# Fourteen modulation loads with buffers from the start, and the relative-bias staging moved to the fourth block of stage 1

## The chip, the cores and the metric

The kernel runs on one core of one Trainium2 chip. The metric is the time of one execution on the device in microseconds (us); the kernel before was run three times.

## What is computed

One layer of a streaming trunk, in float32, for a prompt of 2048 tokens and eight sample streams of 16 tokens. Cut to what matters here:

```
m = silu(c) @ w_mod + b_mod                  # six sections of 1024 columns; sections 0 and 1 are needed first
h = rmsnorm(x) * (1 + scale1) + shift1
proj = h @ w_in                              # columns shared out between two groups
group A: causal conv of width 4 + silu on q, k, v; gated delta rule; gated norm
group B: banded attention, scores + rel_bias[:, clip(qpos - kpos)]
x = x + gate1 * (concat(o_A, o_B) @ w_out)
x = x + gate2 * relu(norm(x) * (1 + scale2) + shift2) ** 2 @ w_down     # through w_up
```

## The kernel before

The program has two stages. Stage 1 goes over six blocks of two or three tiles of 128 tokens (`BLOCKS1`; the third tile of the first block holds the samples). Stage 2 does the attention, the output projection and the FFN. A scheduler in the framework orders the instructions of each engine from the code's order and its own model of times; the order is fixed when the program is built. Large matrices are multiplied in three matmuls of split halves (lines 162 to 164, or three lines of their own in a group's loop), so each weight tile is loaded (`raw`, L174), cast by ScalarE (`w`, L175), and its low half is made by GpSimd (`w`, L82 on POOL). In the first block the cast weights are also stored (`s_w_in`, L183), and later blocks load them back (L178) beside fresh `raw` loads.

All loads and stores of this case are issued by SyncE (SP), in one queue in program order. An issue waits for what its buffer needs and, through one of eight semaphores used in turn, for the DMA issued eight before it.

**The start.** `modulation_start` loads sixteen pieces of `w_mod` of 512 KB (`raw` on L281). Each pair of pieces feeds eight matmuls into `mps` (L287), an add into `rows` (L82), and small transposes `ptm` (L316). Nine buffers (`NPRE`) hold the pieces, so the tenth load waits until the first piece has been multiplied. The three `x` tiles of the first block are loaded on L260, after every fourth piece. `conv_consts` then loads three groups of conv weights and histories (`cwt`, two small DMAs each, L450 and L451), transposes each in eight small matmuls (`psc`, L454 and L455), and copies them out on VectorE (`cw`, `hists`). When the modulation and these are done, `htmp`/`hT` are made, and TensorE starts with `psg` (264 columns, the gates) and `psq` (384 columns, q/k/v for the conv).

**Each block.** The conv of group A is VectorE and ScalarE work per column group (`pre`, `hist`, `y`); the delta rule of each block runs in generators that the scheduler mixes with the next projections. The `x` tiles of the next block are loaded (L372) and normed (`bst` is the statistics of a tile on VectorE, L377) ahead of time.

**The relative biases.** `rel_bias` runs once, when block index 1 begins. It loads 8 rows (`ext`, L1095), reverses and extends them by two copies on VectorE (L1097, L1098), stores them (`s_ext`, L1099), and spreads them by two DMAs from DRAM to DRAM: `s_bias`, 2560 KB (L1100), and `s_bs`, 264 KB (L1101). Stage 2 reads these.

Of the kernel before, what the change touches and what calls it, by code (L numbers as in the profile page):

```python
# [8 lines left out]
F32 = mybir.dt.float32  # L9
# [5 lines left out]
P = 128  # L15
D = 1024
# [19 lines left out]
NT2 = max(len(b) for b in BLOCKS2)  # L36
LATE = (4, 2)
GP = 3
NPRE = 9


def bcast(ap, axis, n):
# [9 lines left out]
class Trunk:  # L52
# [167 lines left out]
    def modulation_start(self, first, tiles, p0):  # L220

        nc, i = self.nc, self.i
        R = 1 + NB
        self.modT = self.const.tile([P, 4, KT, R], F32, name="modT")
        self.cT = self.p1.tile([P, KT, 32], F32, name="cT")
        crow = p0.tile([P, D], F32, name="crow")[0:R]
        nc.sync.dma_start(crow[0:1], i["c_prompt"])
        nc.sync.dma_start(crow[1:R], i["c_sample"])
        load = lambda n: self.mod_load(*first[n], p0.tile([P, D], F32, tag="raw0", name="raw0", bufs=NPRE))
        rvs, xs = [], []  # L230
        for n in range(min(NPRE, len(first))):
            rvs.append(load(n))
            if n == 1:
                gains = p0.tile([16, P], F32, name="gains")
                nc.sync.dma_start(gains[0:8], i["norm1_g"][0].rearrange("(a b) -> a b", b=P))
                nc.sync.dma_start(gains[8:16], i["norm2_g"][0].rearrange("(a b) -> a b", b=P))
                rows = p0.tile([P, 2, D], F32, name="rows")
                nc.gpsimd.memset(rows, 0.0)
                for k, sec in enumerate(dict.fromkeys(c[0] for c in first)):
                    nc.sync.dma_start(rows[0:R, k], dram_ap(i["b_mod"], sec * D, [[0, R], [1, D]]))  # L240
        th = p0.tile([P, D], F32, name="cth")[0:R]
        self.act(th, crow, AF.Tanh, scale=0.5)
        self.ts(crow, crow, 0.5, ALU.mult)
        self.stt(crow, th, 1.0, crow, ALU.add, ALU.mult)
        pt = self.pa.tile([P, 512], F32, tag="pa", name="pt")
        for k in range(KT):
            nc.tensor.transpose(pt[:, k * R:(k + 1) * R], crow[:, k * P:(k + 1) * P], self.ident[0:R, 0:R])
        nc.vector.memset(self.cT, 0.0)
        nc.vector.tensor_copy(self.cT[:, :, 0:R], pt[:, 0:KT * R].rearrange("p (k r) -> p k r", r=R))
        self.rowT = self.const.tile([P, 16], F32, name="rowT")  # L250
        pr = self.pa.tile([P, 512], F32, tag="pa", name="ptr")
        nc.tensor.transpose(pr[:, 0:16], gains, self.ident[0:16, 0:16])
        nc.vector.tensor_copy(self.rowT, pr[:, 0:16])
        order = list(dict.fromkeys(c[0] for c in first))
        for n, (sec, q, u) in enumerate(first):
            if n + NPRE < len(first):
                rvs.append(load(n + NPRE))
            if n % 4 == 3 and len(xs) < len(tiles):
                x = self.hp.tile([P, D], F32, tag="x", name="x", bufs=self.nx)
                nc.sync.dma_start(x, self.x_src(tiles[len(xs)]))  # L260
                xs.append(x)
            if u == 0:
                ps = self.gp.tile([P, 512], F32, tag="g", name="mps")[:, 0:256]
            self.mod_mm(ps, rvs[n], u, u == 0, u == 1)
            if u:
                row = rows[:, order.index(sec), q * 256:(q + 1) * 256]
                self.tt(row, row, ps, ALU.add)
                self.mod_finish(sec, q, row, self.gp, "g")
        self.conv_consts(p0)
        return xs  # L270
# [168 lines left out]
    def conv_consts(self, p0):  # L439
        nc, c, i = self.nc, self.p1, self.i  # L440

        self.cw = c.tile([P, 12, 4], F32, name="cw")
        self.hist = c.tile([P, 12, 3], F32, name="hist")
        nc.vector.memset(self.hist, 0.0)
        self.hists = c.tile([P, 12, NB * 3], F32, name="hists")
        for g in range(3):
            gs = slice(g * 512, (g + 1) * 512)
            t = p0.tile([24, D], F32, tag="cwt", name="cwt", bufs=3)
            w4, h24 = t[0:4, 0:512], t[0:24, 512:1024]
            nc.sync.dma_start(w4, i["conv_w"][0][:, gs])  # L450
            nc.sync.dma_start(h24, i["state_conv"][0].rearrange("b w c -> (b w) c")[:, gs])  # L451
            ps = self.pa.tile([P, 512], F32, tag="pa", name="psc")
            for k in range(4):
                nc.tensor.transpose(ps[:, k * 4:(k + 1) * 4], w4[:, k * P:(k + 1) * P], self.ident[0:4, 0:4])  # L454
                nc.tensor.transpose(ps[:, 64 + k * 24:64 + (k + 1) * 24], h24[:, k * P:(k + 1) * P], self.ident[0:24, 0:24])  # L455
            self.ts(self.cw[:, 4 * g:4 * g + 4], ps[:, 0:16].rearrange("p (k r) -> p k r", r=4), 0.5, ALU.mult)
            nc.vector.tensor_copy(self.hists[:, 4 * g:4 * g + 4], ps[:, 64:160].rearrange("p (k r) -> p k r", r=24))
# [570 lines left out]
    def phase1(self):  # L1028
        nc, tc = self.nc, self.tc
        with ExitStack() as st:  # L1030
            P_ = lambda name, **kw: st.enter_context(tc.tile_pool(name=name, bufs=1, **kw))
            right = ExitStack()
            R_ = lambda name, bufs=1, **kw: right.enter_context(tc.tile_pool(name=name, bufs=bufs, side="right", **kw))
            self.p1, self.hp, self.qp = (P_(x) for x in ("p1c", "p1h", "p1q"))
            self.bp = R_("p1b")
            self.ps = R_("p1ps", 3, space=bass.MemoryType.PSUM)
            pst = ExitStack()
            self.pa = pst.enter_context(tc.tile_pool(name="p1pa", bufs=5 - GP, side="right", space=bass.MemoryType.PSUM))
            self.patag = "pa"
            self.nt = max(len(b) for b in BLOCKS1)  # L1040
            self.nx, self.nA, self.inplace = 3, 4, True
            self.hT = self.p1.tile([P, KT, 2, self.nt * P], F32R, name="hT1")
            with tc.tile_pool(name="p0", bufs=1, side="right") as p0:
                xs = self.modulation_start([(sec, q, u) for q in range(4) for sec in (1, 0) for u in range(2)],
                                           BLOCKS1[0], p0)
            self.mod_todo = [(sec, q, u) for sec in (2, 3, 4, 5) for q in range(4) for u in range(2)]
            self.tp = R_("p1t")
            self.cp = pst.enter_context(tc.tile_pool(name="p1a", bufs=1, side="right"))
            self.phase1_consts()
            S0 = self.tp.tile([P, AH, P], F32, tag="S", name="S", bufs=1)  # L1050
            nc.vector.memset(S0, 0.0)
            self.S = S0
            B = BLOCKS1
            ca = lambda b: 24 * (512 + 1536) * len(B[b])
            cb = lambda b: 24 * 1536 * len(B[b])
            last = len(B) - 1
            self.load_hT(B[0], xs, 0, 1)
            for bi, tiles in enumerate(B):
                self.bi = bi
                self.keep["w_in"] = bi == 0  # L1060
                if bi == 1:
                    self.rel_bias()
                self.drain_to(bi - 2)
                blk = self.proj_a(tiles, self.hT, B[bi + 1] if bi in LATE else ())
                if bi == last:
                    break
                self.gdn(blk, tiles, bi)
                self.pace(0.95 * (cb(bi) * (bi not in LATE) + ca(bi + 1)), 6000)
                if bi not in LATE:
                    self.proj_b(tiles, self.hT, B[bi + 1])  # L1070
            pst.close()
            self.pa = R_("p1pa2", 1, space=bass.MemoryType.PSUM)
            self.ap2 = R_("p1att", 1, space=bass.MemoryType.PSUM)
            self.ap = R_("p1at")
            self.queue(self.attention_first(BLOCKS2[0]), 1 + BH + BH // 2 * len(BLOCKS2[0]) + BH + 2, lane=2)
            self.queue(self.conv_gen(), 6, lane=1)
            self.gdn(blk, tiles, last)
            rest = [last] + list(LATE)
            self.pace(0.85 * sum(cb(b) for b in rest))
            for b, nb in zip(rest, rest[1:] + [None]):  # L1080
                self.proj_b(B[b], self.hT, B[nb] if nb is not None else ())
            self.drain()
            nc.sync.dma_start(self.o["gdn_prompt"][0, 0].rearrange("h k v -> k h v"), self.S)
            right.close()
# [506 lines left out]
```

## Time and profile before

| | |
|---|---|
| median of 3 runs | 3227.69 us (3222.45 to 3229.71) |
| the profiled execution | 3216.33 us, span 3214.6 us |
| TensorE busy, share of the span | 95% |
| VectorE, ScalarE, GpSimd | 56%, 46%, 19% |
| mean granted TensorE clock | 0.979 of full speed |
| DMA | 751.69 MB, mean 234 GB/s |

The profile is one execution. It was 11.4 us faster than the median of the three timed runs, so a sum of changes is made against 3216.33 us and then carried to the median. PE is TensorE's matmul part, DVE VectorE, ACT ScalarE, POOL GpSimd, SPq the queue of SyncE. The granted clock is given as a share of full speed: 1.00 is 2.4 GHz and 0.50 is 1.2 GHz.

### The profile page before, as it was taken

The page shows a single profiled execution, that of the slowest core. Times are in us where ns is not written, and L with a number is a line of the kernel's source. Part 1 is how long each engine was busy: PE and PEld are TensorE (multiplying, and loading weights), DVE is VectorE, ACT ScalarE, POOL GpSimd, SP SyncE. Part 2 cuts the span into 40 slices and gives each one's busy share as a digit, 9 for nine tenths or more (in the row PEclk, how much of TensorE's full clock was granted, in tenths as well). Part 3 has the DMA queues.
Part 4 walks back from the last instruction along what each step waited for, and adds up shares of the span by engine and source line. Part 5 has one row for each costly group of instructions (what it writes and reads, how often), then busy time and mean ns, then how long its engine had stood idle before and what let it go on. Part 6 is the DMA issues. An engine that isn't in the chain of part 4 may idle for free.

```text
span 3214.6 us, 53090 instructions
## 1 busy us (share of the span) xinstructions
PE 3059.3 (95%) x19577; PEld 2704.5 (84%) x19577; DVE 1805.8 (56%) x4526; ACT 1479.9 (46%) x2707; POOL 599.3 (19%) x521
## 2 busy tenths in 40 slices
PE   7899999999999979989999999999999999998998
PEld 5798988898989968878888888888888887787997
DVE  5975777767868654778225556244556433243223
ACT  3554544556655645655434435344434433333332
POOL 4641312121222247631122210000000000000000
PEclk9999999999989989989999999999999999999999
DMA  9789897878897778884655666566675676677876
GB/s 292 221 269 280 265 291 220 269 234 254 270 305 248 233 239 264 258 293 157 193 191 190 208 227 216 178 198 194 197 254 186 214 228 222 224 245 227 254 245 197
DMA packets 630268, 751.69 MB, mean 234 GB/s; under 512 B 59680, under 2 KB 483728, under 8 KB 627960
## 3 DMA queue, kind: packets, MB, share of 16 engines
q1 hardware_dynamic: 624248, 716.84, 70.4%
q0 software_dynamic: 5760, 31.46, 2.9%
q8 instruction: 154, 2.52, 0.3%
q14 instruction: 106, 0.87, 0.1%
HBM read 635.55 MB, written 115.52 MB: 234 GB/s over the span
## 4 chain that ended last, share of the span: by engine, by line
PE 70%; DMA 13%; DVE 11%; issue 2%; ACT 2%; POOL 2%; SPq 1%; ACTq 0%; POOLq 0%; DVEq 0%
PE psu L1479 7%; PE psd L164 7%; PE psd L162 7%; PE psu L1480 7%; PE psu L1481 7%; PE psd L163 7%; DMA x<-in_x_prompt_dram 2%; PE psb L163 2%; PE psb L162 2%; PE psb L164 2%; PE psq L520 1%; PE psq L521 1%; PE psq L519 1%; PE psS L1267 1%; PE pv L1285 1%
## 5 line engine op out<-in xcount | busy, mean ns | idle before, releaser
L175 ACT CAST w<-raw 128x1024 fp32r<-128x1024 f32 (+1 forms) x528 | 552.5, 1048 | 356.4 <-PE psd L164 178.1
L1479 PE MATMUL psu<-hT,w 128*128 128x512 f32 (+2 forms) x1304 | 467.9, 360 | 5.6 <-ACT hT L104 5.6
L1480 PE MATMUL psu<-hT,w 128*128 128x512 f32 (+2 forms) x1304 | 466.6, 358 | 1.9 <-DVE r L89 1.4
L1481 PE MATMUL psu<-hT,w 128*128 128x512 f32 (+2 forms) x1304 | 465.4, 357 | 0.6 <-POOL w L82 0.6
L162 PE MATMUL psd<-w,u 128*128 128x512 f32 x1088 | 431.2, 396 | 0.7 <-DVE u L82 0.7
L164 PE MATMUL psd<-w,u 128*128 128x512 f32 x1088 | 429.8, 396 | 0.0
L163 PE MATMUL psd<-w,u 128*128 128x512 f32 x1088 | 426.6, 392 | 0.0
L82 POOL TENSOR_TENSOR w<-raw,w 128x1024 fp32r<-128x1024 f32 (+1 forms) x132 | 317.6, 2415 | 301.5 <-ACT w L175 232.4
L79 DVE SCALAR_TENSOR_TENSOR psu<-psu,r 128x512 f32<-128x512 f32 (+2 forms) x160 | 98.8, 617 | 417.0 <-ACT r L92 417.0
L82 DVE TENSOR_TENSOR y<-y,psd 128x512 f32<-128x512 f32 x238 | 162.5, 685 | 251.2 <-PE psd L164 250.5
L1479 PEld LDWEIGHTS psu<-hT,w 128*128 128x128 f32 x1304 | 245.4, 189 | 39.2 <-ACT hT L104 6.5
L1481 PEld LDWEIGHTS psu<-hT,w 128*128 128x128 f32 x1304 | 245.8, 189 | 33.7 <-POOL w L82 0.8
L1480 PEld LDWEIGHTS psu<-hT,w 128*128 128x128 f32 x1304 | 246.0, 189 | 33.3 <-DVE hT L82 2.5
L92 ACT ACTIVATE r<-psu 128x512 f32<-128x512 f32 (+2 forms) x160 | 85.5, 534 | 375.6 <-issue 209.8
L164 PEld LDWEIGHTS psd<-w,u 128*128 128x128 f32 x1088 | 204.2, 188 | 46.6 <-DVE u L82 0.3
L163 PEld LDWEIGHTS psd<-w,u 128*128 128x128 f32 x1088 | 204.6, 188 | 45.7 <-issue 1.9
L162 PEld LDWEIGHTS psd<-w,u 128*128 128x128 f32 x1088 | 204.4, 188 | 44.1 <-DVE u L82 1.5
L162 PE MATMUL psb<-w,hT 128*128 128x256 f32 x816 | 236.1, 290 | 0.4 <-ACT qraw L976 0.4
L164 PE MATMUL psb<-w,hT 128*128 128x256 f32 x816 | 234.1, 288 | 0.5 <-DVE hT L82 0.5
L163 PE MATMUL psb<-w,hT 128*128 128x256 f32 x816 | 233.3, 287 | 0.0
L519 PE MATMUL psq<-hT,w 128*128 128x384 f32 (+1 forms) x576 | 193.2, 336 | 0.9 <-ACT pres L534 0.9
L520 PE MATMUL psq<-hT,w 128*128 128x384 f32 (+1 forms) x576 | 193.3, 336 | 0.0
(318 smaller groups left out, 6566.7 us busy)
## 6 DMA issues: line engine op xcount, KB each, us to landing
raw<-in_w_up_dram SPq DMA_DIRECT2D x160, 512.0 KB
raw<-in_w_down_dram SPq DMA_DIRECT2D x160, 512.0 KB
raw<-in_w_in_dram SPq DMA_DIRECT2D x156, 512.0 KB
w<-s_w_in SPq DMA_DIRECT2D x130, 512.0 KB
w<-s_w_down SPq DMA_DIRECT2D x128, 512.0 KB
w<-s_w_up SPq DMA_DIRECT2D x96, 512.0 KB
raw<-in_w_out_dram SPq DMA_DIRECT2D x40, 512.0 KB
x<-in_x_prompt_dram SPq DMA_DIRECT2D x38, 512.0 KB
```

Of the source, the lines that this page charges most:

```text
L79: (eng or self.nc.vector).scalar_tensor_tensor(out, in0, scalar, in1, op0, op1)
L82: (eng or self.nc.vector).tensor_tensor(out, in0, in1, op)
L92: self.nc.scalar.activation(out, in_, func, **kw)
L162: mm(out, lh, rh, start=first, stop=False)
L163: mm(out, lh, rl, start=False, stop=False)
L164: mm(out, ll, rh, start=False, stop=last)
L175: nc.scalar.copy(w[:, 0, 0:n], r)
L519: mm(ps[:, 0:T], wh, hT[:, k, 0, 0:T], start=(k == 0), stop=False)
L520: mm(ps[:, 0:T], wh, hT[:, k, 1, 0:T], start=False, stop=False)
L1479: mm(ps[:, c0:c1], wh, h2[:, k, 0, c0:c1], start=(k == 0), stop=False)
L1480: mm(ps[:, c0:c1], wh, h2[:, k, 1, c0:c1], start=False, stop=False)
L1481: mm(ps[:, c0:c1], wl, h2[:, k, 0, c0:c1], start=False, stop=(k == KT - 1))
```

## The change

Three things change in the code of the start, and one in the loop over blocks. `NPRE` goes from 9 to 12, and two more pieces of `w_mod` go into the two buffers of another pool (tag `big`), so fourteen loads are issued without a wait for a buffer, and the last two after the first and the second multiplication. The three `x` loads are issued between them. The conv constants have one buffer in place of three (`cwt`), and the scratch `cth` of the silu shares it. And `rel_bias`, whose `ext` uses a buffer of the tag `big` too, is called at block index 3 instead of 1.

```
-NPRE = 9
+NPRE = 12
...
-        load = lambda n: self.mod_load(*first[n], p0.tile([P, D], F32, tag="raw0", name="raw0", bufs=NPRE))
         rvs, xs = [], []
-        for n in range(min(NPRE, len(first))):
-            rvs.append(load(n))
+
+        def load(n):
+            pool, tag, bufs = (self.hp, "big", 2) if n in (NPRE, NPRE + 1) else (p0, "raw0", NPRE)
+            rvs.append(self.mod_load(*first[n], pool.tile([P, D], F32, tag=tag, name="raw0", bufs=bufs)))
+
+        for n in range(min(NPRE + 2, len(first))):
+            load(n)
+            if n % 4 == 3 and len(xs) < len(tiles):
+                x = self.hp.tile([P, D], F32, tag="x", name="x", bufs=self.nx)
+                nc.sync.dma_start(x, self.x_src(tiles[len(xs)]))
+                xs.append(x)
...
-        th = p0.tile([P, D], F32, name="cth")[0:R]
+        th = p0.tile([24, D], F32, tag="cwt", name="cth", bufs=1)[0:R]
...
-            if n + NPRE < len(first):
-                rvs.append(load(n + NPRE))
-            if n % 4 == 3 and len(xs) < len(tiles):
-                x = self.hp.tile([P, D], F32, tag="x", name="x", bufs=self.nx)
-                nc.sync.dma_start(x, self.x_src(tiles[len(xs)]))
-                xs.append(x)
             if u == 0:
                 ps = self.gp.tile([P, 512], F32, tag="g", name="mps")[:, 0:256]
             self.mod_mm(ps, rvs[n], u, u == 0, u == 1)
+            if n + NPRE + 2 < len(first):
+                load(n + NPRE + 2)
...
-            t = p0.tile([24, D], F32, tag="cwt", name="cwt", bufs=3)
+            t = p0.tile([24, D], F32, tag="cwt", name="cwt", bufs=1)
...
-                if bi == 1:
+                if bi == 3:
                     self.rel_bias()
```

The change adds four lines ahead of most of the code, so a line of the kernel before stands four higher afterwards (L450 becomes L454).

SyncE's queue at the start. Before, the conv constants (`cwt`) are issued among the `w_mod` pieces, soon after the `x` tiles:

```order
L260 DMA x<-in_x_sample_dram 128x1024
L450 DMA cwt<-in_conv_w_dram 4x512
L451 DMA cwt<-in_state_conv_dram 24x512
L450 DMA cwt<-in_conv_w_dram 4x512
L451 DMA cwt<-in_state_conv_dram 24x512
L281 DMA raw_169<-in_w_mod_dram 128x4x256
L450 DMA cwt<-in_conv_w_dram 4x512
L281 DMA raw_176<-in_w_mod_dram 128x4x256
L451 DMA cwt<-in_state_conv_dram 24x512
```

The same queue of the changed kernel, from the last piece of `w_mod` on; five small constants (gdng, qkg twice, alog, dtb) stand between the first pair of `cwt` loads and the first rows of `w_in`, and are not shown:

```order
L174 DMA raw<-in_w_in_dram 128x4x264 x2
L174 DMA raw<-in_w_in_dram 128x8x128
L454 DMA cwt<-in_conv_w_dram 4x512
L455 DMA cwt<-in_state_conv_dram 24x512
L183 DMA s_w_in<-w 128x1056
L454 DMA cwt<-in_conv_w_dram 4x512
L455 DMA cwt<-in_state_conv_dram 24x512
L174 DMA raw<-in_w_in_dram 128x8x128
```

All sixteen pieces and the three `x` tiles now stand ahead of any `cwt` load; the second `cwt` group stands behind three `w_in` loads, and the third behind a store that waits for GpSimd.

VectorE, around the statistics (`bst`) of the third `x` tile of the second block. Before, they stand after the first group of the conv (`hist`, `y`):

```order
L529 COPY hist<-pre 128x3
L535 COPY hists<-pres 128x24
L79 SCALAR_TENSOR_TENSOR y<-pre,cw,y 128x256
L79 SCALAR_TENSOR_TENSOR y<-pres,cw,y 128x128
L79 SCALAR_TENSOR_TENSOR y<-pre,cw,y 128x256
L79 SCALAR_TENSOR_TENSOR y<-pres,cw,y 128x128
L79 SCALAR_TENSOR_TENSOR y<-pre,cw,y 128x256
L79 SCALAR_TENSOR_TENSOR y<-pres,cw,y 128x128
L527 COPY pre<-hist 128x3
L533 COPY pres<-hists 128x8x3
L377 BN_STATS bst<-x 128x6 x2
L79 SCALAR_TENSOR_TENSOR sgw<-th,psg 128x256
```

In the changed kernel:

```order
L79 SCALAR_TENSOR_TENSOR sgw<-th,psg 128x256
L381 BN_STATS bst<-x 128x6 x2
L382 BN_AGGR bmv<-bst 128x2
L82 TENSOR_TENSOR hT_98<-htmp,hT_98 128x4x128
L382 BN_AGGR bmv<-bst 128x2
L79 SCALAR_TENSOR_TENSOR ss<-bmv 128x1 x2
L89 TENSOR_SCALAR r<-ss 128x1 x2
L79 SCALAR_TENSOR_TENSOR sgw<-th,psg 128x256
L533 COPY hist<-pre 128x3
L539 COPY hists<-pres 128x24
```

The third statistics now stand ahead of the first conv group, and ahead of one `hT` of the first block.

SyncE's queue where the third block ends and the fourth begins. Before:

```order
L281 DMA rawx<-in_w_mod_dram 128x4x256 x2
L501 DMA s_sg<-sgw 128x256
L296 DMA mrow<-in_b_mod_dram 9x256
L560 DMA s_vt<-kvw 128x128 x3
L178 DMA w<-s_w_in 128x1024
L501 DMA s_sg<-sgw 128x256
L281 DMA rawx<-in_w_mod_dram 128x4x256
L174 DMA raw<-in_w_in_dram 128x8x128
L560 DMA s_kt<-kvw 128x128 x3
L372 DMA x<-in_x_prompt_dram 128x1024
```

In the changed kernel:

```order
L285 DMA rawx<-in_w_mod_dram 128x4x256
L1103 DMA s_ext<-ext 8x768
L285 DMA rawx<-in_w_mod_dram 128x4x256
L505 DMA s_sg<-sgw 128x256
L1104 DMA s_bias<-s_ext 1024x1x640
L1105 DMA s_bs<-s_ext 128x1x528
L300 DMA mrow<-in_b_mod_dram 9x256
L564 DMA s_vt<-kvw 128x128 x3
L285 DMA rawx<-in_w_mod_dram 128x4x256
L505 DMA s_sg<-sgw 128x256
L564 DMA s_kt<-kvw 128x128 x3
L376 DMA x<-in_x_prompt_dram 128x1024
```

The two DRAM to DRAM transfers now stand ahead of `mrow` and of the first `x` load of the fourth block (`rawx` are later pieces of `w_mod`; `mrow` is their bias row).

## Rows read from the trace of the kernel before

**Rows 1.** The page: the span, and busy time with shares and instructions of each engine.

```profile
span 3214.6 us, 53090 instructions
...
PE 3059.3 (95%) x19577; PEld 2704.5 (84%) x19577; DVE 1805.8 (56%) x4526; ACT 1479.9 (46%) x2707; POOL 599.3 (19%) x521
```

**Rows 2.** Windows: length; busy PE, PEld, DVE, ACT, POOL (instructions); granted clock; DMA share; GB/s.

```profile
20.00:40.00 20.00, 15.07 (x124) 8.90 (x115) 10.26 (x37) 7.69 (x10) 3.71 (x4) 0.97 0.96 296
40.00:60.00 20.00, 12.74 (x76) 11.18 (x77) 17.12 (x33) 8.94 (x16) 9.47 (x7) 0.69 0.84 274
...
80.00:100.00 20.00, 13.81 (x71) 13.18 (x70) 19.85 (x53) 9.64 (x22) 12.38 (x7) 0.91 0.71 216
...
220.00:320.00 100.00, 100.00 (x765) 88.37 (x764) 60.92 (x178) 51.05 (x101) 10.90 (x14) 1.00 0.96 294
```

**Rows 3.** The chain that ended last, first 140 us: start, length, what.

```profile
14.35 9.48 DMA raw<-in_w_mod_dram
...
61.76 13.64 DMA x<-in_x_prompt_dram
```

**Rows 4.** SyncE's timeline at the start: start, length, queue, line, operation.

```profile
16.25 0.34 SPq L450 DMA_DIRECT2D cwt<-in_conv_w_dram  x1
...
29.99 3.15 SPq L174 DMA_DIRECT2D raw<-in_w_in_dram  x3
...
35.45 0.37 SPq L281 DMA_DIRECT2D raw<-in_w_mod_dram  x1
...
49.06 1.90 SPq L1100 DMA_DIRECT2D s_bias<-s_ext  x1
51.01 8.12 SPq L1101 DMA_DIRECT2D s_bs<-s_ext  x1
...
61.76 5.70 SPq L372 DMA_DIRECT2D x<-in_x_prompt_dram  x1
```

**Rows 5.** TensorE's timeline at the start; in brackets idle before and what ended it.

```profile
25.68 0.26 PE L454 MATMUL psc<-ident,cwt 4*128 4x4 f32 x1 [0.85 <-DMA cwt<-in_conv_w_dram]
...
41.65 1.08 PE L287 MATMUL mps<-raw,cT 128*32 128x256 f32 x8 [2.88 <-DMA raw<-in_w_mod_dram]
...
48.03 0.57 PE L162 MATMUL psg<-w,hT 128*128 128x264 f32 x1
```

**Rows 6.** ScalarE's timeline, its first instruction.

```profile
3.16 1.28 ACT L92 ACT_TABLE_LOAD   x1 [3.16 <-DMA crow<-in_c_sample_dram]
```

**Rows 7.** VectorE's timeline, 40 to 76 us.

```profile
40.33 2.60 DVE L1097 COPY ext<-ext 8x320 f32<-8x320 f32 x1 [2.16 <-DMA ext<-in_rel_bias_dram]
42.85 2.48 DVE L1098 COPY ext<-ext 8x384 f32<-8x384 f32 x1
...
67.79 1.60 DVE L529 COPY hist<-pre 128x3 f32<-128x3 f32 x1 [6.87 <-ACT pre L528]
...
75.42 1.28 DVE L377 BATCH_NORM_STATS2 bst<-x 128x6 f32<-128x512 f32 x2 [3.77 <-DMA x<-in_x_prompt_dram]
```

**Rows 8.** SyncE's timeline where the third block ends.

```profile
495.42 0.46 SPq L501 DMA_DIRECT2D s_sg<-sgw  x1
500.12 0.31 SPq L296 DMA_DIRECT2D mrow<-in_b_mod_dram  x1
...
504.48 0.38 SPq L281 DMA_DIRECT2D rawx<-in_w_mod_dram  x1
...
507.43 0.41 SPq L372 DMA_DIRECT2D x<-in_x_prompt_dram  x1
```

**Rows 9.** Windows while `s_bias` moves, and at the end of the third block.

```profile
48.00:60.00 12.00, 10.07 (x61) 9.39 (x62) 9.50 (x25) 5.51 (x11) 4.34 (x4) 0.82 0.82 260
496.00:516.00 20.00, 19.11 (x223) 15.81 (x222) 13.73 (x42) 8.65 (x20) 6.52 (x6) 1.00 0.82 251
516.00:532.00 16.00, 13.85 (x119) 12.58 (x118) 14.77 (x43) 9.12 (x20) 5.59 (x8) 1.00 0.46 135
```

**Rows 10.** TensorE's timeline, first gate matmul of the fourth block.

```profile
527.17 0.37 PE L162 MATMUL psg<-w,hT 128*128 128x264 f32 x1
```

## The prediction

> **What bounds the kernel now.** I read the page first. TensorE is busy for 95% of the span and no other engine for more than 56% [rows 1], so only time in which TensorE idles can be won, some 155 us in all. Then I cut the span into windows, since the change acts in two places only. In the first stretch TensorE is far from full: 15.07 us busy of 20 between 20 and 40 us, 12.74 of 20 in the next, 13.81 of 20 between 80 and 100; from 220 to 320 it is full [rows 2]. The same rows say what limits it. From 20 to 40 us the DMA is at a share of 0.96 and moves 296 GB/s: the modulation waits for its weights. From 80 to 100 us VectorE is busy for 19.85 of 20 us: there the conv on VectorE sets the pace. Between the two, from 40 to 60 us, the clock is at 0.69 on the mean, that is partly at 1.2 GHz, because TensorE idled just before.
>
> The chain of waits names the links: a `w_mod` load for 9.48 us, and later an `x` load that takes 13.64 us from 61.76 us on [rows 3]. The timelines place them. The last `w_mod` pieces reach TensorE at 41.65 us after a wait of 2.88, and the first gate matmul starts at 48.03 [rows 5]. VectorE stands 2.16 us for `ext`, then makes two small copies of 2.60 and 2.48 us, and at 75.42 us starts the statistics of a third `x` tile after 3.77 us of waiting for its DMA [rows 7]. That load was issued only at 61.76, behind `s_bs`, whose issue holds SyncE for 8.12 us [rows 4].
>
> **Term 1: the start up to the first gate matmul.** In the changed order all sixteen pieces of `w_mod` and three `x` tiles are issued without a gap, 19 loads of 0.524 MB, 9.96 MB. At the 296 GB/s of [rows 2] that is 33.7 us; with the 1.5 us that pass before the first is issued (an estimate from the first rows of the queue) the last lands at about 35 us instead of 41.6. That is 6 us won for the modulation, but the conv constants now come behind it, and the gate matmuls stand behind all three groups in TensorE's order. The first group lands with the last weights, at 35. The second is issued behind three `w_in` loads, 1.6 MB or 5.4 us at the same rate: 40 us. The third waits for the transposes of the second and for a store behind GpSimd's first low half, and then lands between two bounds. Short: the very first loads of the program were in by 3.16 us [rows 6], so at most 3.2 us, at 43. Long: a `cwt` load of before was issued at 16.25 [rows 4] and used at 25.68 [rows 5], 9.4 us behind a full queue, at 49. From there on its transposes, the copies on VectorE and the last `htmp` and `hT` take about 4.5 us (an estimate: from 41.65 to 48.03 is 6.4 us, with part of the `ext` copies in it). The first gate matmul comes between 46 us (if the second group too is quick) and 53.5. The queue is nearly empty when the third group is issued, so I take the nearer end and a little more: 48.5, **0.5 us later** than before; the ends are 2 us earlier and 5.5 later. So the earlier modulation brings nothing here: the wait for `w_mod` turns into a wait for `cwt`.
>
> On this the Trainium skill has a rule, page "DMA: Bandwidth & Descriptors", section "Rules for kernel authors": many small transfers should be made one, since under 64 KB one pays mostly overhead; a group here is 8 KB and 48 KB. The section "Anatomy of one DMA" gives about 2 us of fixed cost, and the first rows of this trace agree as far as they go, with 3.16 us for two small loads and what stands ahead of them. By that figure the third group would land at 42, the gate matmuls would start at 46.5, and the sum below would end 2 us lower; the sum itself goes by the rows.
>
> **Term 2: the third `x` tile.** `rel_bias` leaves the second block: its two copies, its 10.0 us of SyncE (1.90 and 8.12 [rows 4]) and 2.9 MB of traffic. The third `x` load of the second block is then no longer behind them, and the order puts its statistics ahead of the first conv group, where VectorE idles 6.87 us before 67.79 [rows 7]. So the stall of 3.77 and the 1.28 us of statistics leave the stretch where VectorE is full. **Minus 5.0 us**, if the stretch behind it moves as a whole; the windows say it can, since VectorE is 19.85 of 20 us busy and the DMA at 0.71 [rows 2]. The ends: 0, if it is GpSimd's low halves and the `w_in` stream that pace this stretch, and 5.0. Removing the `ext` copies wins nothing more, as they lie ahead of the first gate matmul, which term 1 holds.
>
> **Term 3: the end of the third block.** There `s_bias` and `s_bs` now stand in SyncE's queue after an `s_sg` that ended at 495.88, ahead of `mrow` at 500.12 and the first `x` load of the fourth block at 507.43 [rows 8]. With 10.0 us of issue `mrow` leaves at about 506, 5.9 us later, and so at most do the pieces and `x` tiles behind it. The fourth block's first gate matmul was at 527.17 [rows 10], behind the norm of those tiles. TensorE already idles there, 0.9 us of the 20 up to 516 and 2.1 of the next 16 [rows 9], and in the new order steps of the delta rule move ahead of the transposes of `x` and fill some of the wait. Then the traffic: 2.9 MB at the 260 GB/s that moved while it ran before [rows 9] is 11.1 us of all DMA. Up to 516 us the share of 0.82 leaves 3.6 us, so 7.5 us of it run over into the next window, which at 0.46 has room for 8.6. The ends are 0 (all behind other work) and 13.4 (5.9 and 7.5 one behind the other). I take **4.0 us**, two thirds of the 5.9: the block is short of neither VectorE nor `w` at that moment, but the norm of `x` is the next thing that TensorE needs. The `ext` load and copies come earlier, where nothing waits for them, and cost nothing as long as VectorE has its gaps there (13.73 busy of 20 [rows 9]); without them, up to the 5.1 us of [rows 7].
>
> **The sum.** 0.5 - 5.0 + 4.0 = -0.5 us. Against the profiled execution 3216.3 becomes 3215.8. That execution was 11.4 us under the median of 3227.69, so on the median the forecast is **3227 us**. About 0.2%, 6.4 us, is what a measurement of this kernel can tell from no change.
>
> **The rivals.**
> - *Both short ends, faster.* The third `cwt` group is quick and TensorE starts 2 us earlier, and the DMAs at the end of the third block hide behind the delta rule: -2.0 - 5.0 + 0 = -7.0, 3221 us. For it: TensorE idles so little before 516 us that there is work to put in. Against it: the second group stands behind 1.6 MB.
> - *The end of the third block decides, slower.* If queue and traffic add up, 13.4 us: 0.5 - 5.0 + 13.4 = +8.9, 3237 us. It decides from 10.9 us of lost TensorE time there. For it: in the second block a load issued behind the same two transfers took 13.64 us [rows 3]. Against it: the room of 8.6 us just after.
> - *The third statistics block VectorE, slower.* They now stand ahead of one `hT` of the first block and of the first conv group. If the tile landed as late as 75.4, as before, the conv would start 7.6 us later than 67.79, nothing of term 2 would come, and the sum is 0.5 + 7.6 + 4.0 = +12.1, 3240 us. It decides from a landing 2 us after the conv could start. Against it: without `s_bs` ahead of it the load should be issued some 10 us earlier.
> - *Nothing reaches TensorE.* The stretch from 60 to 140 us is paced by GpSimd and the weights, and term 3 is hidden as well: 0.5 us, 3228 us, no change.
>
> **How the numbers follow.** My sum and its neighbours within 0.2% get 0.35, nothing at all 0.11, the faster rival 0.28, the end of the third block 0.16, the third statistics 0.10. So faster 0.28, same 0.46, slower 0.26. The range takes in the cases from 3221 to 3240 and, on the low side, as much below as the unknown ends and the 7 us between three timed runs make likely: 3214 to 3240. The likeliest case alone reaches from 3221 to 3234.
>
> **What would show it.** In the changed kernel's trace: the last `mps` at about 36 us and not at 41.65; TensorE waiting for `psc` or `htmp` after it, with the first gate matmul near 48.5; no wait for `x` on VectorE near 70 us, and the conv groups after the first 5 us earlier, with a block 1 that starts 4 to 5 us earlier; around 500 us SyncE held 10 us by two issues, and the first gate matmul of the fourth block at most 5 us ahead of, or level with, 527.17. I am wrong if the first gate matmul comes near 43 or 53, if the lead at 220 us is gone, or if TensorE loses over 10 us around 515.

## The result, and the profile after

The changed kernel is slower: 3240.24 us median of 8 runs (3233.37 to 3245.46), against 3221.84 us for the kernel before in 8 runs (3215.68 to 3229.75). The ratio is 1.0057, 95% interval 1.0045 to 1.0069, or 18 us. The forecast was no change, 3227 us.

The page of the changed kernel, as in [rows 1]:

```profile
span 3234.9 us, 53085 instructions
...
PE 3069.1 (95%) x19577; PEld 2718.3 (84%) x19577; DVE 1799.3 (56%) x4526; ACT 1479.1 (46%) x2707; POOL 602.8 (19%) x521
```

TensorE has the same 19577 instructions. Its busy time is 9.8 us longer and its idle time 10.5 us, so the loss is idle time and time at the lower clock. To place it I compare the start of the first gate matmul (`psg`, 264 columns) of a block in the two timelines. In the profiled execution of the kernel before these are at 48.03, 219.73, 398.62, 527.17, 720.02 and 812.61 us for blocks 0 to 5, and the span is 3214.6. In the changed kernel they are at 50.93, 221.32, 400.06, 544.00, 729.53 and 821.71, and the span is 3234.9. So it is 2.9 us behind at the start, 1.6 at block 1, 1.4 at block 2, 16.8 at block 3, **9.5 at block 4**, 9.1 at block 5 and **20.3 at the end**.

The mark at block 3 has to be read with care. With `rel_bias` there the scheduler puts other work of TensorE ahead of this gate matmul: 3523 matmuls stand ahead of it in the kernel before, 3553 in the changed kernel, 3577 in e1 below. At blocks 2 and 4 the count is the same in both kernels. The windows from the gate matmul of block 2 to that of block 4 (length; busy PE, PEld, DVE, ACT, POOL; granted clock; DMA share; GB/s), before and after:

```profile
398.62:720.02 321.40, 310.23 (x2419) 280.26 (x2418) 243.06 (x738) 157.95 (x322) 73.40 (x73) 0.98 0.83 255
400.06:729.53 329.47, 310.14 (x2419) 282.28 (x2417) 244.79 (x747) 159.67 (x323) 74.34 (x73) 0.97 0.84 258
```

So 8.1 us are lost around block 3, and a second loss, 11 us in these two executions, arises behind block 5.

SyncE's timeline of the changed kernel at the start, as in [rows 4]:

```profile
33.53 1.48 SPq L174 DMA_DIRECT2D raw<-in_w_in_dram  x3
35.11 0.75 SPq L454 DMA_DIRECT2D cwt<-in_conv_w_dram  x1
...
41.17 0.36 SPq L183 DMA_DIRECT2D s_w_in<-w  x1
42.14 0.26 SPq L454 DMA_DIRECT2D cwt<-in_conv_w_dram  x1
...
42.84 0.39 SPq L174 DMA_DIRECT2D raw<-in_w_in_dram  x1
```

TensorE's timeline of the same stretch, as in [rows 5]:

```profile
35.22 1.94 PE L291 MATMUL mps<-raw,cT 128*32 128x256 f32 x16
...
40.98 0.26 PE L458 MATMUL psc<-ident,cwt 4*128 4x4 f32 x1 [2.26 <-DMA cwt<-in_conv_w_dram]
...
44.25 0.24 PE L458 MATMUL psc<-ident,cwt 4*128 4x4 f32 x1 [2.14 <-DMA cwt<-in_conv_w_dram]
...
50.08 1.11 PE L349 MATMUL psh<-ident,x 128*128 128x128 f32 x4 [2.07 <-ACT htmp L92]
50.93 0.59 PE L162 MATMUL psg<-w,hT 128*128 128x264 f32 x1
```

ScalarE there, the fourth cast of `w_in`:

```profile
47.68 1.04 ACT L175 CAST w<-raw 128x1024 fp32r<-128x1024 f32 x1 [5.72 <-DMA raw<-in_w_in_dram]
```

The last pieces of `w_mod` are multiplied from 35.22 us on (the last eight matmuls from 36.1), six us earlier than before. Then TensorE waits for the second `cwt` group and for the third. Behind them ScalarE stands 5.72 us for the fourth `w_in` load, which is issued only after the third group; `htmp` is queued behind that cast, and the first gate matmul starts at 50.93.

SyncE where the third block ends, as in [rows 8]:

```profile
499.82 0.73 SPq L1104 DMA_DIRECT2D s_bias<-s_ext  x1
500.61 5.39 SPq L1105 DMA_DIRECT2D s_bs<-s_ext  x1
506.10 1.43 SPq L300 DMA_DIRECT2D mrow<-in_b_mod_dram  x1
...
519.19 0.38 SPq L376 DMA_DIRECT2D x<-in_x_prompt_dram  x1
```

VectorE there:

```profile
518.52 0.42 DVE L82 TENSOR_TENSOR mrow<-mrow,mps 128x256 f32<-128x256 f32 x1 [7.33 <-DMA mrow<-in_b_mod_dram]
518.86 1.12 DVE L79 SCALAR_TENSOR_TENSOR X<-kS,neg,X 128x128 f32<-128x128 f32 x4
```

And TensorE:

```profile
519.26 1.01 PE L838 MATMUL pY<-X,A 128*128 128x128 f32 x3 [6.98 <-DVE X L79]
```

`mrow` is 9 KB. Issued at 506.10 behind the two DRAM to DRAM transfers, it lands 12.4 us later. Its add stands in front of `X` of the delta rule on VectorE, and TensorE waits 6.98 us for `X`. The first `x` of the fourth block is issued at 519.19, 11.8 us later than in [rows 8].

### The profile page after: what moved, and what is told of

Its sections match the earlier page's. It is cut to its first block, busy times and chain, and to the rows that moved or that the text cites. A ratio compares the mean times of both kernels' runs of the same rounds, so it can differ in the third digit from the quotient of the medians.

```text
span 3234.9 us, 53085 instructions
## 1 busy us (share of the span) xinstructions
PE 3069.1 (95%) x19577; PEld 2718.3 (84%) x19577; DVE 1799.3 (56%) x4526; ACT 1479.1 (46%) x2707; POOL 602.8 (19%) x521
## 4 chain that ended last, share of the span: by engine, by line
PE 71%; DMA 12%; DVE 10%; ACT 2%; issue 2%; POOL 2%; SPq 1%; ACTq 0%; POOLq 0%; DVEq 0%
PE psu L1483 7%; PE psu L1484 7%; PE psu L1485 7%; PE psd L164 7%; PE psd L162 7%; PE psd L163 7%; DMA raw<-in_w_up_dram 2%; DVE y L79 2%; PE psb L163 2%; PE psb L162 2%; PE psS L1271 2%; PE pso L162 2%; PE psb L164 2%; PE pso L163 2%; PE psq L525 2%
```

## The experiments

Each run was timed in five rounds with the kernel before on the same chip: e1 to e4, e9 and e10 on one chip, e5 to e8 on a second, e11 and e12 on a third. The lags are in us behind the profiled execution of the kernel before, at the first gate matmul of blocks 0 to 5 and at the end of the span; those at block 3 can be compared only between runs with the same work ahead of that matmul. They are single executions: e2, e11 and e12 have the same order of instructions up to about 900 us and differ by 8 us at block 5; and the profiled execution of before was faster than its median, that of e8 11 us slower than its own. So totals go by the medians and ratios, and the lags tell places to some 5 us only.

| run | median us | ratio to before, 95% | block 0 | 1 | 2 | 3 | 4 | 5 | end |
|---|---|---|---|---|---|---|---|---|---|
| changed kernel | 3240.24 | 1.0057 (1.0045 to 1.0069) | 2.9 | 1.6 | 1.4 | 16.8 | 9.5 | 9.1 | 20.3 |
| e1 move only | 3219.95 | 0.9994 (0.9978 to 1.0009) | -3.2 | -6.6 | -7.8 | 6.1 | -1.4 | -1.0 | -3.0 |
| e2 start only | 3238.08 | 1.0055 (1.0037 to 1.0072) | 3.7 | 6.5 | 6.3 | 6.9 | 8.9 | 8.8 | 18.1 |
| e3 pair on ScalarE's queue | 3253.23 | 1.0102 (1.0079 to 1.0125) | 2.8 | 2.5 | 2.3 | 18.4 | 10.6 | 10.7 | 41.5 |
| e4 pair on GpSimd's queue | 3235.41 | 1.0044 (1.0029 to 1.0060) | 3.1 | 4.1 | 3.3 | 21.8 | 11.9 | 9.7 | 17.3 |
| e5 three cwt buffers | 3241.05 | 1.0064 (1.0043 to 1.0085) | 0.6 | 0.9 | 1.0 | 17.5 | 10.4 | 12.1 | 29.2 |
| e6 move, one cwt buffer | 3232.19 | 1.0038 (1.0024 to 1.0052) | 5.6 | 3.4 | 3.6 | 17.0 | 15.9 | 18.3 | 18.6 |
| e7 changed, other pace | 3239.12 | 1.0053 (1.0032 to 1.0073) | 3.5 | 4.5 | 3.8 | 18.2 | 10.1 | 10.6 | 28.5 |
| e8 before, other pace | 3223.69 | 1.0014 (0.9995 to 1.0034) | -1.4 | -0.6 | 0.2 | 0.5 | 1.9 | 2.1 | 17.8 |
| e9 move to index 4 | 3217.19 | 0.9989 (0.9975 to 1.0003) | -3.4 | -6.6 | -7.2 | 0.2 | 9.2 | 7.8 | 3.6 |
| e10 before, delayed | 3234.85 | 1.0042 (1.0026 to 1.0058) | 7.1 | -0.9 | 1.0 | 9.6 | 11.4 | 14.2 | 26.3 |
| e11 start only, pace 0.84 | 3228.88 | 1.0031 (1.0015 to 1.0047) | 4.1 | 6.6 | 6.0 | 3.0 | 4.7 | 4.6 | 10.5 |
| e12 start only, pace 0.80 | 3238.02 | 1.0062 (1.0039 to 1.0085) | 3.9 | 6.3 | 5.5 | 10.7 | 12.9 | 12.9 | 31.0 |

**e1, the move alone.** The kernel before with one line changed:

```
-                if bi == 1:
+                if bi == 3:
```

> The kernel before, with rel_bias called at block index 3 and nothing else changed. Theory A (the two DRAM to DRAM transfers at the end of the third block cost most of the 18 us): between 8 and 16 us slower than before, with VectorE waiting at least 5 us for mrow near 515 us and TensorE idle behind it. Theory B (the loss comes from the new start, or from the order of the instructions everywhere): within 6 us of before, no such wait for mrow.

The wait for `mrow` came as theory A said; here TensorE lost 6.3 us behind it. VectorE's row and TensorE's:

```profile
508.12 0.88 DVE L82 TENSOR_TENSOR mrow<-mrow,mps 128x256 f32<-128x256 f32 x2 [5.91 <-DMA mrow<-in_b_mod_dram]
509.05 1.03 PE L316 MATMUL ptm<-sel,mrow 128*128 128x9 f32 x4 [6.29 <-DVE mrow L82]
```

But the time did not change. Without the `ext` copies the first gate matmul comes 2.6 us after the last `mps`, on TensorE:

```profile
42.22 1.08 PE L287 MATMUL mps<-raw,cT 128*32 128x256 f32 x8 [2.18 <-DMA raw<-in_w_mod_dram]
...
44.85 0.57 PE L162 MATMUL psg<-w,hT 128*128 128x264 f32 x1
```

The kernel is 6.6 us ahead at block 1, 7.8 at block 2 and 1.4 at block 4. The window between the last two, to be held against the two in the section on the result:

```profile
390.84:718.63 327.79, 311.15 (x2419) 281.95 (x2417) 242.45 (x746) 159.07 (x323) 74.78 (x73) 0.97 0.83 259
```

It is 6.4 us longer than before, about TensorE's wait behind `mrow`. (The 6.1 us behind at block 3 hold 54 matmuls that in the kernel before come later.) Theory A falls as the cause of the 18 us: the transfers cost some 6 us where they stand, and the move as a whole costs nothing.

**e2, the start alone.** The changed kernel with `rel_bias` at index 1:

```
-                if bi == 3:
+                if bi == 1:
```

> The changed kernel with rel_bias back at block index 1, so the buffers and the conv constants are changed alone. Theory A: first gate matmul near 51 us, 0 to 6 us slower than before, no loss at 500 to 545 us. Theory B: 10 us slower or more.

Theory B: nearly all of the loss is here, 17.7 us by the ratio and 14.5 by the medians. It is 6.5 us behind at block 1, and in this variant VectorE shows the third rival of the prediction, the statistics ahead of the first conv group:

```profile
70.48 1.29 DVE L381 BATCH_NORM_STATS2 bst<-x 128x6 f32<-128x512 f32 x2 [4.34 <-DMA x<-in_x_prompt_dram]
...
75.95 1.29 DVE L381 BATCH_NORM_STATS2 bst<-x 128x6 f32<-128x512 f32 x2 [2.85 <-DMA x<-in_x_prompt_dram]
77.16 1.69 DVE L533 COPY hist<-pre 128x3 f32<-128x3 f32 x1
```

The first conv group starts at 77.16 instead of 67.79. In the changed kernel, with the transfers gone from here, it starts at 71.74. Another 9 us are lost behind block 5 in this execution.

**e3 and e4, the pair in another queue.** The two transfers of the changed kernel issued by ScalarE (e3, shown), and by GpSimd (e4, the same with `nc.gpsimd`):

```
-        nc.sync.dma_start(self.s_bias, dram_ap(self.s_ext, P, [[EXT, BH], [-1, P], [1, 640]]))
+        nc.scalar.dma_start(self.s_bias, dram_ap(self.s_ext, P, [[EXT, BH], [-1, P], [1, 640]]))
-        nc.sync.dma_start(self.s_bs, dram_ap(self.s_ext, P, [[EXT, BH], [-1, SL], [1, 528]]))
+        nc.scalar.dma_start(self.s_bs, dram_ap(self.s_ext, P, [[EXT, BH], [-1, SL], [1, 528]]))
```

> The changed kernel with s_bias and s_bs issued by ScalarE's queue and not by SyncE's. Theory A1 (the small mrow load stands behind 2.9 MB in one queue): mrow lands within 4 us of its issue, TensorE's idle time near 515 us falls from 7 us to under 2, 8 to 12 us faster than the changed kernel. Theory A2 (the DMA engines are taken whichever queue issues): mrow still takes 8 us or more, within 4 us of the changed kernel.

> The changed kernel with s_bias and s_bs issued by GpSimd. Theory A1: mrow lands within 4 us, 8 to 12 us faster than the changed kernel, less what the issue costs GpSimd (the spans of GpSimd's own work tell). Theory A2: mrow takes 8 us or more, within 4 us of the changed kernel.

In e4 `mrow` was issued on SyncE at 507.36 and VectorE had it at 522.65, 15 us later, although nothing of the pair stood in that queue. SyncE's timeline of e4:

```profile
507.36 0.37 SPq L300 DMA_DIRECT2D mrow<-in_b_mod_dram  x1
```

and VectorE's, with the add for it:

```profile
522.65 0.42 DVE L82 TENSOR_TENSOR mrow<-mrow,mps 128x256 f32<-128x256 f32 x1 [6.62 <-DMA mrow<-in_b_mod_dram]
```

Theory A1 fails: without the pair in its queue the small load took no less. That it waits for the DMA engines, as A2 has it, is the rival that is left and was not tested by itself. By the medians the run is 4.8 us faster than the changed kernel, where A2 said at most 4 and A1 8 to 12, and the two intervals overlap. (Not every DMA of this program is issued by SyncE: in stage 2, far behind this place, GpSimd issues 40 loads of `KV`.) In e3 the issue itself held ScalarE, whose rows are

```profile
500.98 6.76 ACTq L1105 DMA_DIRECT2D s_bs<-s_ext  x1
507.86 0.48 ACT L561 COPY kvw<-ptq 128x384 f32<-128x384 f32 x1 [7.81 <-issue]
```

so the 8.3 us lost between blocks 2 and 4 have another cause here. The 13 us by which its median is above that of the changed kernel were foreseen by neither theory; the profiled execution lost them behind block 5.

**e5, early loads with three `cwt` buffers.** The changed kernel with

```
-NPRE = 12
+NPRE = 10
...
-            t = p0.tile([24, D], F32, tag="cwt", name="cwt", bufs=1)
+            t = p0.tile([24, D], F32, tag="cwt", name="cwt", bufs=3)
```

(and `cth` in the same three).

> The changed kernel with three buffers for cwt and cth again, and ten of the pieces of w_mod in raw0 in place of twelve (the same space; twelve loads at once with the two of the tag big). Theory S (the single cwt buffer costs the start): first gate matmul at 42 to 46 us, and 6 to 10 us ahead of the changed kernel at 500 us. Rival E (issuing the w_mod loads early costs the start): still 50 us or later. Its order at the end of stage 1 is that of the changed kernel; theory O (that order costs 6 to 9 us between 900 and 1300 us) says that this part of the loss stays, theory L (the loss there comes of being late) that it goes.

Theory S said 42 to 46 us for the first gate matmul, rival E 50 or later; it came at 48.63, between the two. At block 2 the run is 0.4 us ahead of the changed kernel and not 6 to 10, and the time is the same. Behind block 5, where its order is that of the changed kernel, the loss stays (17 us in this execution), as theory O said. TensorE no longer waits for `cwt` at the end but for `htmp`:

```profile
45.81 1.12 PE L349 MATMUL psh<-ident,x 128*128 128x128 f32 x4 [4.22 <-ACT htmp L92]
48.63 0.59 PE L162 MATMUL psg<-w,hT 128*128 128x264 f32 x1 [1.70 <-ACT hT L104]
```

because two of VectorE's copies between the `htmp` last more than 2.3 us,

```profile
42.56 2.39 DVE L531 COPY pre<-hist 128x3 f32<-128x3 f32 x1
44.87 0.40 DVE L89 TENSOR_SCALAR htmp<-psh,modT 128x128 f32<-128x128 f32 x1
45.19 2.33 DVE L537 COPY pres<-hists 128x24 f32<-128x24 f32 x1
```

while GpSimd makes the first low halves of `w_in`:

```profile
40.12 7.12 POOL L82 TENSOR_TENSOR w<-raw,w 128x1056 fp32r<-128x1056 f32 x3 [9.66 <-ACT w L175]
```

Most copies of 3 columns take 0.16 us in these traces. With the move alone (e1) the first gate matmul was at 44.85. So the single buffer is not the only cost; loading early costs as well.

**e6, the move with one `cwt` buffer.** e1, and

```
-            t = p0.tile([24, D], F32, tag="cwt", name="cwt", bufs=3)
+            t = p0.tile([24, D], F32, tag="cwt", name="cwt", bufs=1)
```

> The kernel before with rel_bias at block index 3, and with one buffer for cwt in place of three; nine w_mod loads at once as before. Theory S: first gate matmul 4 us or more later than with the move alone (44.85 us), 3 to 10 us slower than it at 500 us. Rival E: within 2 us of the move alone. Its order at the end of stage 1 is another one than that of the changed kernel; theory O: no loss of 6 us or more between 900 and 1300 us.

Theory S holds here: 53.58 us, behind

```profile
48.63 0.26 PE L454 MATMUL psc<-ident,cwt 4*128 4x4 f32 x1 [6.45 <-DMA cwt<-in_conv_w_dram]
```

and its median is 12 us above that of e1. It is 18.3 us behind at block 5 and 18.6 at the end, and only 9.9 by the medians, so in this run being late is not paid again.

**e7 and e8, another order of the transition.** In the changed kernel and in the kernel before:

```
-            self.pace(0.85 * sum(cb(b) for b in rest))
+            self.pace(0.84 * sum(cb(b) for b in rest))
```

> The changed kernel with 0.84 in place of 0.85 as the pacing factor of the last projections of stage 1: the order of the instructions is the same up to about 900 us and differs in the transition to stage 2. Theory O: still 9 us behind the kernel before at 900 us, then 0 to 4 us lost in the transition instead of 8, so 4 to 10 us faster than the changed kernel. Theory L: within 3 us of the changed kernel.

> The kernel before with 0.84 in place of 0.85 as the same factor. Theory O: equal to the kernel before up to 900 us, then up to 8 us away from it on either side. Theory L: within 3 us.

Both medians stayed within 2 us of their parents. For e7 theory O fails. For e8 it had allowed anything up to 8 us, so that run decides little.

**e9, the move to index 4.** As e1, with `bi == 4`.

> The kernel before with rel_bias called at block index 4, nothing else changed. If the first stage's lead of some 7 us (as with the move to index 3) stays, and what the two transfers take at the end of the third block is not taken elsewhere: 4 to 8 us faster than before, with the first gate matmul at 45 us and no wait of more than 4 us for mrow or x behind the transfers. If they take the same wherever a block ends, within 4 us of the move to index 3 and of before.

The first stage's lead is there again (6.6 us at block 1, 7.2 at block 2) and `mrow` is not waited for. But 7.4 us are lost up to block 3, where no transfer stands now: TensorE's granted clock is 0.50 (1.2 GHz) from 480 to 500 us, against 0.83 in the kernel before. Before, then e9:

```profile
480.00:500.00 20.00, 16.40 (x162) 13.40 (x162) 10.88 (x30) 7.62 (x18) 1.27 (x2) 0.83 0.85 263
480.00:500.00 20.00, 18.49 (x128) 15.24 (x129) 7.44 (x20) 5.73 (x15) 1.36 (x2) 0.50 0.61 179
```

Another 9 us are lost up to block 4, and there the pair does at its new place what it did at the old one. A store of `kTs`, issued at 659.63 behind `s_bias`, holds its buffer until 675.64, ScalarE waits for it and TensorE for ScalarE:

```profile
675.64 0.59 ACT L1012 CAST kTs<-ptk 128x512 fp32r<-128x512 f32 x1 [7.96 <-DMA s_kv<-kTs]
676.28 0.75 PE L1011 MATMUL ptk<-identr,stk 128*128 128x128 f32 x4 [5.61 <-ACT kTs L1012]
```

The interval reaches to 1.0003: not told apart from before, and the version that would beat both kernels was not found.

**e10, a delay.** The kernel before with, ahead of the conv constants,

```
+        ps = self.gp.tile([P, 512], F32, tag="g", name="dly")
+        for _ in range(64):
+            nc.tensor.transpose(ps[:, 0:P], rows[:, 1, 896:D], self.ident)
```

> The kernel before with 64 transposes of the finished modulation rows put ahead of the first gate matmul on TensorE, which nothing reads: a delay of the first gate matmul, with w_mod, cwt and w_in loaded as before. Theory L (a late start is paid more than once, as the loss of the changed kernel grows from 9 us at 900 us to 18 at the end): the time grows by more than 1.5 times the lag at 140 us. Theory P (a late start is paid once or less): by the lag at 140 us or less, and then the second half of the loss has another cause.

TensorE's timeline:

```profile
46.04 8.44 PE L271 MATMUL dly<-ident,rows 128*128 128x128 f32 x64
54.31 1.04 PE L348 MATMUL psh<-ident,x 128*128 128x128 f32 x8
55.10 0.37 PE L162 MATMUL psg<-w,hT 128*128 128x264 f32 x1
```

and the windows (length, busy time of PE, PEld, DVE, ACT, POOL, then the granted clock, the DMA share and GB/s):

```profile
50.00:60.00 10.00, 10.00 (x89) 10.00 (x88) 8.04 (x17) 2.55 (x6) 2.16 (x3) 1.00 0.72 267
60.00:80.00 20.00, 20.00 (x126) 19.76 (x126) 10.14 (x29) 10.20 (x20) 11.79 (x8) 1.00 0.93 317
```

The gate matmuls start 7.1 us late, but at a granted clock of 1.00 (2.4 GHz; TensorE was busy with the transposes just before) and without a gap up to 80 us; the first conv group starts at 68.80, and at block 1 the kernel is 0.9 us ahead. So the lag there is nothing, theory P, and yet the time is 0.42% longer: all of it is lost from block 2 on, where the scheduler wrote another order from about 500 us on. That the order does it is argued, not shown.

**e11 and e12, the start alone in two more orders of the transition.** e2 with 0.84, and with 0.80, as in e7.

> The start alone (as e2) with 0.84 as the pacing factor: the order up to about 900 us is that of e2, the transition to stage 2 is written in another order. Theory O (the order that the change happens to get there costs 6 to 8 us, and another order can cost less): the same 9 us behind before at 900 us, and 5 us or more faster than e2 at the end. Theory L (a start that is late by as much always costs that): within 3 us of e2, 13 to 19 us slower than before.

> The same with 0.80, a third order of the transition. Theory O: a time of its own, 5 us or more away from e2 or from the run at 0.84. Theory L: within 3 us of both.

e11 is 9.2 us faster than e2 by the medians, with the same order up to about 900 us; they were timed on two chips, and the intervals of their ratios overlap. The stronger comparison is e11 with e12, timed together: 9.1 us, and their orders differ almost only between 1000 and 1300 us. That is theory O as it was put for e12, and theory L fails there. The median of e12 is that of e2. The windows from 920 to 1320 us of the kernel before, the changed kernel, e11 and e12, in this order:

```profile
920.00:1320.00 400.00, 362.85 (x2839) 336.62 (x2840) 261.98 (x735) 227.60 (x470) 166.61 (x121) 0.94 0.78 246
920.00:1320.00 400.00, 360.38 (x2779) 335.45 (x2779) 253.46 (x736) 222.91 (x464) 152.89 (x114) 0.92 0.79 245
920.00:1320.00 400.00, 359.77 (x2845) 334.78 (x2844) 261.31 (x741) 227.60 (x472) 160.49 (x119) 0.95 0.78 248
920.00:1320.00 400.00, 351.46 (x2738) 328.66 (x2739) 253.28 (x717) 219.34 (x456) 151.07 (x115) 0.92 0.77 243
```

The two slower ones get 60 and 107 matmuls less done here, in part because they come late into the window, and at a lower granted clock. A clock 0.02 lower over 400 us is 8 us of full-speed time (an estimate from these rows), about the size of the loss; whether the clock makes the loss or idle time in the order brings the clock down was not tested. It is not the whole of it: over their timed runs the mean granted clock is 0.974 in the changed kernel, but 0.977 in e2 as in the kernel before.

The lag that is added between block 5 and the end is 6 to 18 us in e2, e7, e11 and e12, and 0.3 us in e6, which was the latest of all at block 5. That speaks against lateness as the cause, but it is a hint: e8 adds 15.7 us there in its profiled execution and 1.4 in the median.

## Why the prediction was wrong

**Term 1 failed, "0.5 us later than before".** As the start alone it is 1.0055, 18 us (12 to 23). The steps up to the landing of the constants were right to 1.3 us: last `mps` forecast at 36 us and at 36.1; second `cwt` group at 40 and at 40.98; third at 43 and at 44.25. Wrong were three things behind them.
- The tail from the third group to the first gate matmul was put at 4.5 us and was 6.7. ScalarE's order, with the fourth `w_in` cast ahead of `htmp`, was in the program to be read; the load itself is issued behind the third `cwt` group, at 42.84, and was cast at 47.68.
- The comparison was wrong. The forecast counted the earlier `w_mod` as a gain that the `cwt` wait takes away. In the kernel before, the conv constants and the first `htmp` and `hT` are made while the last pieces of `w_mod` are under way: e1 needs only 2.6 us from the last `mps` to the first gate matmul, the changed kernel 14.9 from its own (36.1 to 50.93). Loading `w_mod` first brings it in 6 us earlier and moves most of this work behind it, where it also meets GpSimd's low halves. Against e1 the changed kernel is 6.1 us behind at the first gate matmul and 8.2 at block 1, and e2 against the kernel before 3.7 and 6.5: that is what the start costs where it stands. Of the forecast's own signs of being wrong, the lost lead at 220 us came true.
- It was summed as if nothing behind the start would change. Nearly half of the loss, 9 to 11 us in the profiled executions of e2 and the changed kernel and 6 to 9 if the medians are taken for the end, arises behind block 5, in an order of instructions that these two and e5 share from about 900 us to the end of stage 1. e11 has the same start as e12 in another order and is 9 us faster. That an order there can cost this much is shown; that it is the order's doing in the changed kernel is not, as e7 changed it and won nothing.

**Term 2 was too small.** Forecast minus 5.0 us; the move alone leads by 6.6 at block 1, in e1 and in e9. The forecast held that removing the `ext` copies wins nothing more, since they lie ahead of the first gate matmul; e1 won 3.2 us there, and 3.4 in the stretch that the 5.0 were meant for. VectorE's wait of 3.77 us for the third `x` [rows 7] is gone in both.

**Term 3 was too small at its place, and waited for the wrong thing.** `mrow` was forecast to leave at "about 506" and left at 506.10, which was luck: the pair was issued at 499.82, some 4 us later than the forecast had it, and held SyncE 6.3 us instead of 10.0. 4.0 us were taken, and 6.4 (e1) and 8.1 (changed kernel) were lost between blocks 2 and 4, most of them TensorE's waits of 6.3 and 7.0 us behind `mrow`. These are single executions: e10 and e12, without the transfers there, lost 10.4 and 7.4 us in the same stretch. The step that failed is that the norm of `x` was taken to be next in need: it was `mrow`, which landed 12.4 us after its issue (in the kernel before its add ran 4.4 us after the issue and waited for TensorE, not for the load), and the add stands ahead of the delta rule on VectorE. The sum of terms 2 and 3, minus 1.0, is about what the move alone did, minus 2 us, 0.9978 to 1.0009; that is luck too, as both terms were too small and their errors cancel.

Put together from e2 and e1, the start costs 6.5 us, the move wins 6.6 by block 1 and loses 6.4 around block 3. That makes 6.3 at block 4, against 9.5 in the changed kernel, which is as near as single executions come. The rest, behind block 5, stood in no term.

**The rivals.** The slower rival at the end of the third block needed 10.9 us of lost TensorE time there; 8.1 were lost, so it came near at that place and was not the cause. The one on the third statistics came true in e2 and in e11 and e12, which have its order there (first conv group at 77.16, 77.45 and 76.36), and not in the changed kernel. The third group's load took 2.1 us, from 42.14 to 44.25. The page "DMA: Bandwidth & Descriptors" of the Trainium skill (section "Anatomy of one DMA") gives a fixed cost of some 2 us, for DMAs that GpSimd issues, and this load, issued by SyncE, agrees. By its figure the prediction's sum would have ended lower still, so the price of the small load was not what went wrong.

**Open.** Which instructions of the transition make one order dearer than another was not tried, nor was the granted clock there held apart from the order. How e2's 3.7 us at the first gate matmul become 6.5 at block 1, when e10's 7.1 become nothing, is argued from its `x` waits and from e10's clock, not shown by a run of its own.

## What to carry to other kernels

Before work is moved ahead in a queue, list what is done today in the gaps of the thing that is slow: a load that arrives six us sooner gains nothing if those gaps held the work that now follows it. A large DRAM to DRAM transfer should be placed by the smallest load or store that any in-order engine will wait for in the next 15 us; another queue did not help here (e3, e4). A mark in the trace measures a loss only if the same work stands ahead of it in both kernels. And where a scheduler writes the order, a change at the start should be timed against a second draw of the order far behind it, because that can weigh as much as the change.

## What was not expected of the hardware

A 9 KB load took 12.4 to 15.3 us beside DRAM to DRAM transfers of 2.9 MB, from the same queue (changed kernel) and from another (e4), while the DMA share from 500 to 520 us was 0.64 in the changed kernel. In e5 two of VectorE's copies, of 3 and of 24 columns, took 2.39 and 2.33 us instead of 0.16 while GpSimd ran elementwise operations of about 2.4 us on end; a copy of 24 columns at 42.48, between two of these, took 0.17. The Trainium skill, "GPSIMD Engine Reference", section "Specifications", says that the two share their interfaces to SBUF, and the rows of e5 agree; it names contention with VectorE instructions in a 2-port mode or with two SBUF inputs, and whether these copies are of that kind no row here shows.
